# The table of relative biases made in the first stage of a hybrid encoder layer and written to DRAM head by head

## The chip, the cores and the metric

The kernel runs on one core of a Trainium2 chip. The metric is the device time of one execution in microseconds (us). Three runs of the kernel before took 3108.31, 3101.53 and 3108.05 us; the median is 3108.05 us.

## What is computed

One layer with two mixers side by side: a gated delta rule with 16 heads, and a sparse attention with 16 query heads over 2 key and value heads. There are 512 prompt tokens and 64 sample tokens with a past of 1024. Cut to what the change touches:

```python
h = rmsnorm(x, norm_w) * (1.0 + scale[:, None]) + shift[:, None]
proj = h @ w_in                       # 2048 x 16,000 columns, in fp32
(qkv_a, z_a, b_a, a_a, q_b, k_b, v_b, z_b, q_i, k_i, w_i, gl_a, gl_b) = split(proj)

# indexer: scores of all keys, of which the best topk are kept
dots = einsum('bthd,bsd->bths', qi, KI)
score = einsum('bth,bths->bts', wi, relu(dots))
top_val, top_idx = top_k(where(visible, score, -inf), topk)

# attention: the bias depends on the distance of key and query alone
rel = top_idx - q_pos[None, :, None]
bias = rel_bias[rel_bucket(rel)]      # rel_bias is 32 buckets x 16 heads
p = softmax(where(valid, logits + bias, -inf))
o = einsum('btngs,btsnd->btngd', p, Vs)

merged = sigmoid(gl_a) * (o_a @ w_branch_a) + sigmoid(gl_b) * ((o * silu(z_b)) @ w_branch_b)
x = x + gate[:, None] * (merged @ w_out)
```

Keys far enough before the query share the last bucket, so a head's biases are one row of 384 values, shifted by one from query to query, and one constant for keys far away.

## The kernel before

**The tiles.** Every projection is cut into tiles of 128 output columns. A tile loads its weights (`wraw`, 1 MB, line 270, on SP's queue), splits them on ScalarE into a high part (`whi`, line 282) and the negative of it (`wlo`, line 287), and completes the low part by two accumulating transfers of 512 KB each from GpSimd's queue (line 290). `run_tile` (lines 311 to 332) then makes 96 matmuls of 288 columns: 64 of `whi` with the high and the low activations, then 32 of `wlo`. Inside the tile, the weights of the next one are split at the 4th, 14th, 24th and 34th matmul, and those of the third next are loaded at the 84th. The buffers are two deep. In the rows the matmuls are all named `mm`; in the lists of instructions the tile's number stands behind the name (`mm7`, `wraw8`, `whi8`).

**The order.** It is fixed when the program is built. `Plan` keeps a clock of its own for PE (`self.pe`), for each engine and for DMA; each side task is a generator that yields what it waits for, and `tick` runs a task's next step when the plan's clock has come to its due time (lines 129 to 160). `yield 4000` means: 4000 ns later on the plan's clock. These due times only decide in which order instructions are put into the queues. On the chip an instruction starts when its queue has come to it and its semaphores are there.

**SP's queue.** Nearly all transfers are issued by SP, in program order. [...]

**The stages.** The start (adaLN and the normalised activations) is followed by the first stage, `run` from line 1810 on with the pool `p1`: tiles 0 and 1 (keys), 2 (indexer key, `beta` and others), 3 to 10 (indexer queries `qi`), 11 and 12 (values), 13 (a gate). Beside the tiles run `misc` (lines 653 to 743) and the indexer's scores (`score`, lines 817 to 853): nine products `dot` for each of the eight `qi` tiles, through two PSUM buffers that ScalarE empties with a `relu` each. `open_gdn` (line 1730) waits for all of that and opens the delta rule's stage. `open_att` (line 1738) drains the tasks and opens the attention with the pool `p3`.

**The table before.** `bias_setup` (lines 1245 to 1266) is spawned in `open_att`. It loads a one-hot matrix (`oh`) and the 32 by 16 biases (`rb`), makes 16 rows of 512 biases with one product, copies them to SBUF (`f`, named `bf`, 16 partitions), and writes each row's first 384 values 128 times into the DRAM tensor `d_F`, all heads in one transfer (line 1265). Head h's block of keys reads it with a row step of 383 instead of 384, which shifts each row by one (`toeplitz`, line 1268): the tile `BT` in `attend` (line 1311) and `BTs` for the samples (line 1368). `attend` waits for `bias_task` (line 1309). `far` and `fars` hold the constant for far keys. In the attention, `gate_vectors` (line 1477) streams `gada`, 64 pieces of `w_ada`, on the same queue.

Of the kernel before, what the change touches and what calls it, by code (L numbers as in the profile page):

```python
# [7 lines left out]
F32 = mybir.dt.float32  # L8
# [16 lines left out]
H = 16  # L25
# [180 lines left out]
class Kern(Plan):  # L206
# [1037 lines left out]

    def bias_setup(self):

        i, p, V, S = self.i, self.p3, self.V, self.S
        oh = p.tile([32, 512], F32, tag="L3", name="oh", bufs=1)
        S.dma_start(oh, i["k_onehot"])
        rb = p.tile([32, 16], F32, name="rb", bufs=1)  # L1250
        S.dma_start(rb, i["rel_bias"])
        self.far = p.tile([128, 16], F32, name="far", bufs=1)
        S.dma_start(self.far, i["rel_bias"][15:16, :].partition_broadcast(128).rearrange("p a b -> p (a b)"))
        yield [oh, rb, self.far], 9000
        ps = yield from self.tr("biasp")
        self.mm(ps[:16, :], rb, oh)
        f = p.tile([16, 512], F32, tag="PT3", name="bf", bufs=1)
        V.tensor_copy(f, ps[:16, :])
        self.fars = p.tile([128, 8], F32, name="fars", bufs=1)
        v = self.far.rearrange("p (a b) -> p a b", b=2)  # L1260
        for s in range(2):
            V.tensor_copy(self.fars[64 * s:64 * s + 64, :], v[64 * s:64 * s + 64, :, s])
        yield [f]

        S.dma_start(self.d_F, f[:, 0:384].unsqueeze(1).to_broadcast([16, 128, 384]))
        yield [self.d_F]

    def toeplitz(self, h, n, w):

# [36 lines left out]

    def attend(self, a):
        S, p, h = self.S, self.p3, a["h"]
        yield from self.wait(self.kv_task, self.bias_task)
        BT = p.tile([128, 256], F32, tag="BT", name=f"BT{h}")  # L1310
        S.dma_start(BT, self.toeplitz(h, 128, 256))
        yield [BT, a["qT"], a["zt"]]
        yield from self.wait(*[self.spawn(self.attend_block(a, t, BT)) for t in (3, 2, 1, 0)])
        if h % 2:
            a["sample"] = self.spawn(self.attend_sample(h // 2))
# [422 lines left out]
    def open_att(self):  # L1738
        self.drain()
        self.c2.close()  # L1740
        self.c3, self.p3 = self.pool("p3")
        self.slack = 0.0
        self.gpool = lambda: self.p3
        self.bias_task = self.spawn(self.bias_setup())
        self.spawn(self.conv_out())
        self.spawn(self.gate_vectors())
        self.qb_pre(0)()
# [41 lines left out]
    def run(self):  # L1789
        tc = self.tc  # L1790
        with ExitStack() as ctx:
            ctx.enter_context(tc.manual_schedule())
            self.consts(ctx)
            cp = self.cp
            self.wi = cp.tile([128, 4, 16], F32, name="wi")
            self.wis = cp.tile([128, 8], F32, name="wis")
            for n in ("beta", "gc", "egc", "kds"):
                setattr(self, n, cp.tile([128, 5, 16], F32, name=n))
            self.gate = cp.tile([128, KO, 2], F32, name="gate")
            self.diag = cp.tile([128, 64], F32, name="diag")  # L1800
            self.heads, self.att, self.kvT, self.tok = {}, {}, {}, {}
            self.score_tasks, self.topk_task = [], None
            self.topk_gap, self.solve_gap, self.gada_gap = 100, 0, 5000
            self.plan()
            self.hctx = ExitStack()
            pss = self.start(ctx, self.hctx)
            self.catt, self.ap = self.pool("att", bufs=1)
            self.msk = [self.ap.tile([128, 128 * t + 128], F32, name=f"msk{t}") for t in range(4)]
            self.msks = self.ap.tile([128, NS], F32, name="msks")
            self.c1, self.p1 = self.pool("p1")  # L1810
            self.gpool, self.p2 = lambda: self.p1, None
            p = self.p1
            self.kih, self.kil = (p.tile([128, TP + NS], F32R, name=n, bufs=1) for n in ("kih", "kil"))
            self.qss = []
            for b in range(2):
                q = p.tile([128, 2, 128], F32R, name=f"qss{b}", bufs=1)
                self.V.tensor_scalar(q, self.ident.unsqueeze(1).to_broadcast([128, 2, 128]), 0.0, None, op0=ALU.mult)
                self.qss.append(q)
            self.tri = p.tile([128, 2, 128], F32, name="tri", bufs=1)
            self.cache_task = self.spawn(self.cache_idx())  # L1820
            self.load(3)
            for n in range(2):
                for s in range(2):
                    self.stream[n]["epi"](pss[2 * n + s], s)
            self.S.dma_start(self.tri, self.i["k_tri"])
            self.load(4)
            for n in range(2, len(self.stream) - 2):
                self.run_tile(n)
            self.run_last(n + 1)
            self.drain()  # L1830
            for _ in self.finish((2, 3, 4)):
                pass
            for c in (self.c8, self.c6, self.cmg, ):
                c.close()
# [57 lines left out]
```

## Time and profile before

| | |
|---|---|
| median of three runs | 3108.05 us (3101.53 to 3108.31) |
| the profiled execution, whole | 3106.55 us |
| its span, from the first to the last instruction | 3104.8 us |
| PE busy in it | 2972.8 us (96%) |
| VectorE, ScalarE, GpSimd busy | 1389.1, 1542.5, 390.0 us |
| mean granted TensorE clock | 0.977 of full speed |
| first stage, from about | 150 to 357 us |
| attention's opening, about | 1665 to 1750 us |

The profile is of one execution. Its span is 1.75 us shorter than that execution's time. PE is the engine that is nearly always busy, so the time that it stands idle is what other work can cost or give back. In the page's second part the 22nd to 24th of the 40 slices hold the attention's opening.

### The profile page before, as it was taken

The numbers are of one execution on the slowest core, as the hardware profiler recorded it, in microseconds if no ns is written. First come the engines' busy times: TensorE is split into PE (matmuls) and PEld (weight loads), VectorE is DVE, ScalarE is ACT, GpSimd is POOL, SyncE is SP. The second block draws the span as 40 slices with busy tenths as digits, with TensorE's granted clock in tenths as the row PEclk, the third lists the DMA queues.
The fourth block names the chain that finished last, engine by engine and source line by source line (L and its number), as shares of the span: only waits on it lengthen the run. The fifth ranks groups of instructions, "written<-read, shape, count | busy, mean of one in ns | idle before, by whom it ended". The sixth has DMA issues, their size and how long they took to land.

```text
span 3104.8 us, 56419 instructions
## 1 busy us (share of the span) xinstructions
PE 2972.8 (96%) x22363; PEld 2816.3 (91%) x22363; DVE 1389.1 (45%) x4057; ACT 1542.5 (50%) x3332; POOL 390.0 (13%) x727
## 2 busy tenths in 40 slices
PE   6999999999999999999998799999999899999997
PEld 2588999999989989999998699999999899999897
DVE  3334899566667657765651244334422111111112
ACT  3255444555555556665653345444544444444454
POOL 1010111111111111111110000101101111111110
PEclk8999999999999999999999899999999999999999
DMA  9865787766666666676767767776769899888875
GB/s 325 270 147 114 171 185 175 159 162 161 154 144 145 150 145 146 145 167 136 165 153 159 163 160 168 188 177 158 175 148 248 227 234 232 213 209 214 225 159 141
DMA packets 567242, 552.40 MB, mean 178 GB/s; under 512 B 53505, under 2 KB 466066, under 8 KB 565762
## 3 DMA queue, kind: packets, MB, share of 16 engines
q1 hardware_dynamic: 512690, 351.58, 40.1%
q0 software_dynamic: 54144, 197.16, 33.5%
q8 instruction: 176, 2.88, 0.4%
q14 instruction: 88, 0.72, 0.1%
q10 hardware_dynamic: 144, 0.07, 0.0%
HBM read 303.54 MB, written 48.04 MB: 113 GB/s over the span
## 4 chain that ended last, share of the span: by engine, by line
PE 49%; DMA 9%; SPq 3%; ACT 2%; DVE 2%; issue 1%; POOL 0%; ACTq 0%; DVEq 0%; POOLq 0%
PE mm L218 41%; SPq L55 3%; DMA gbl<-d_gb 2%; DMA za<-d_za 2%; DMA wlo<-wraw 2%; PE ob L218 1%; PE lg L218 1%; DMA xf<-in_x_sample 1%; ACT wlo L55 1%; ACT whi L55 1%; PE po L218 1%; PE pT L233 1%; PE obs L218 1%; PE lgs L218 0%; DVE M L55 0%
## 5 line engine op out<-in xcount | busy, mean ns | idle before, releaser
L218 PE MATMUL mm<-hh,whi 128*128 128x288 f32 (+1 forms) x4448 | 1222.3, 301 | 6.1 <-ACT gth L55 5.8
L218 PE MATMUL mm<-hl,whi 128*128 128x288 f32 (+1 forms) x4448 | 1219.8, 300 | 0.0
L218 PEld LDWEIGHTS mm<-hh,whi 128*128 128x128 f32 (+1 forms) x4448 | 839.1, 189 | 22.0 <-issue 9.2
L218 PEld LDWEIGHTS mm<-hl,whi 128*128 128x128 f32 (+1 forms) x4448 | 839.4, 189 | 13.0 <-issue 9.1
L218 PE MATMUL mm<-hh,wlo 128*128 128x288 f32 (+1 forms) x4448 | 685.0, 303 | 4.9 <-DMA wlo<-wraw 4.9
L218 PEld LDWEIGHTS mm<-hh,wlo 128*128 128x128 f32 (+1 forms) x4448 | 619.5, 191 | 13.2 <-DMA wlo<-wraw 5.1
L55 POOL DMA_DIRECT2D wlo<-wraw x376 | 324.3, 863 | 2340.4 <-ACT wlo L55 2062.9
L55 ACT ACTIVATE whi<-wraw 128x512 fp32r<-128x512 f32 x756 | 467.3, 619 | 96.1 <-DMA wraw<-in_w_branch_b 40.2
L55 ACT ACTIVATE wlo<-whi 128x512 fp32r<-128x512 f32 x752 | 475.2, 632 | 70.0 <-PE mm L218 31.6
L55 DVE TENSOR_TENSOR Mt<-M 18x30 f32<-18x30 f32 (+14 forms) x480 | 151.8, 316 | 34.1 <-DMA M<-dN 24.8
L55 DVE TENSOR_TENSOR M<-M,Mt 18x30 f32<-18x30 f32 (+14 forms) x480 | 153.6, 320 | 16.5
L218 PE MATMUL mm<-ga,whi 128*128 128x288 f32 x1024 | 141.1, 297 | 7.1 <-DVE ta L55 6.4
L218 PEld LDWEIGHTS mm<-ga,whi 128*128 128x128 f32 x1024 | 138.3, 190 | 8.2 <-DVE ta L55 7.4
L218 PE MATMUL mm<-mg,whi 128*128 128x288 f32 x1024 | 144.3, 298 | 0.0
L218 PEld LDWEIGHTS mm<-mg,whi 128*128 128x128 f32 x1024 | 139.0, 190 | 0.0
L218 PE MATMUL mm<-gb,whi 128*128 128x288 f32 x1024 | 138.1, 294 | 0.0
L218 PEld LDWEIGHTS mm<-gb,whi 128*128 128x128 f32 x1024 | 136.5, 188 | 0.0
L55 DVE SCALAR_TENSOR_TENSOR cv<-raw,cw,cv 128x579 f32<-128x579 f32 x144 | 117.4, 815 | 4.3 <-ACT cv L55 0.8
L55 DVE SCALAR_TENSOR_TENSOR gacc<-gada,cs,gacc 128x512 f32<-128x512 f32 x120 | 86.6, 744 | 31.1 <-DMA gada<-in_w_ada 31.1
L55 ACT ACTIVATE x<-px 128x128 f32<-128x128 f32 (+1 forms) x80 | 21.9, 274 | 153.4 <-PE px L218 153.4
L55 ACT ACTIVATE raw<-mm 128x288 f32<-128x288 f32 x96 | 36.7, 382 | 99.3 <-PE mm L218 98.4
L55 DVE TENSOR_TENSOR xf<-yp,xf 128x512 f32<-128x512 f32 (+1 forms) x18 | 11.4, 632 | 161.1 <-PE yp L233 134.5
(476 smaller groups left out, 3310.7 us busy)
## 6 DMA issues: line engine op xcount, KB each, us to landing
wlo<-wraw POOLq DMA_DIRECT2D x376, 512.0 KB, 5.4
wraw<-in_w_in SPq DMA_DIRECT2D x140, 1024.0 KB
wa<-in_w_ada SPq DMA_DIRECT2D x64, 512.0 KB
gada<-in_w_ada SPq DMA_DIRECT2D x64, 256.0 KB
wraw<-in_w_branch_a SPq DMA_DIRECT2D x16, 1024.0 KB
wraw<-in_w_branch_b SPq DMA_DIRECT2D x16, 1024.0 KB
wraw<-in_w_out SPq DMA_DIRECT2D x16, 1024.0 KB
d_t<-gth SPq DMA_DIRECT2D x32, 288.0 KB
```

The lines of the kernel that those rows point to most:

```text
L55: r = f(*a, **k)
L218: self.nc.tensor.matmul(out, lhsT, rhs, start=start, stop=stop, **k)
L233: self.nc.tensor.transpose(out, in_, self.ident[:k, :k])
```

## The change

`bias_setup` is spawned in the first stage, before the first tile that `run_tile` handles, and no longer in `open_att`. Its tiles come from the first stage's pool, `far` and `fars` from the constants' pool. The table is written by 16 transfers, one for each head, each from a single partition of `bf`, with a step of 4000 ns on the plan's clock between them. `attend` no longer waits for the task.

```diff
--- before.py
+++ after.py
@@ -1244,26 +1244,26 @@
 
     def bias_setup(self):
 
-        i, p, V, S = self.i, self.p3, self.V, self.S
-        oh = p.tile([32, 512], F32, tag="L3", name="oh", bufs=1)
+        i, p, cp, V, S = self.i, self.p1, self.cp, self.V, self.S
+        oh = p.tile([32, 512], F32, name="oh", bufs=1)
         S.dma_start(oh, i["k_onehot"])
         rb = p.tile([32, 16], F32, name="rb", bufs=1)
         S.dma_start(rb, i["rel_bias"])
-        self.far = p.tile([128, 16], F32, name="far", bufs=1)
-        S.dma_start(self.far, i["rel_bias"][15:16, :].partition_broadcast(128).rearrange("p a b -> p (a b)"))
-        yield [oh, rb, self.far], 9000
+        far = self.far
+        S.dma_start(far, i["rel_bias"][15:16, :].partition_broadcast(128).rearrange("p a b -> p (a b)"))
+        yield [oh, rb, far], 3000
         ps = yield from self.tr("biasp")
         self.mm(ps[:16, :], rb, oh)
-        f = p.tile([16, 512], F32, tag="PT3", name="bf", bufs=1)
+        f = p.tile([16, 512], F32, name="bf", bufs=1)
         V.tensor_copy(f, ps[:16, :])
-        self.fars = p.tile([128, 8], F32, name="fars", bufs=1)
-        v = self.far.rearrange("p (a b) -> p a b", b=2)
+        v = far.rearrange("p (a b) -> p a b", b=2)
         for s in range(2):
             V.tensor_copy(self.fars[64 * s:64 * s + 64, :], v[64 * s:64 * s + 64, :, s])
         yield [f]
 
-        S.dma_start(self.d_F, f[:, 0:384].unsqueeze(1).to_broadcast([16, 128, 384]))
-        yield [self.d_F]
+        for h in range(H):
+            S.dma_start(self.d_F[h], f[h:h + 1, 0:384].unsqueeze(1).to_broadcast([1, 128, 384]))
+            yield 4000
 
     def toeplitz(self, h, n, w):
 
@@ -1306,7 +1306,7 @@
 
     def attend(self, a):
         S, p, h = self.S, self.p3, a["h"]
-        yield from self.wait(self.kv_task, self.bias_task)
+        yield from self.wait(self.kv_task)
         BT = p.tile([128, 256], F32, tag="BT", name=f"BT{h}")
         S.dma_start(BT, self.toeplitz(h, 128, 256))
         yield [BT, a["qT"], a["zt"]]
@@ -1741,7 +1741,6 @@
         self.c3, self.p3 = self.pool("p3")
         self.slack = 0.0
         self.gpool = lambda: self.p3
-        self.bias_task = self.spawn(self.bias_setup())
         self.spawn(self.conv_out())
         self.spawn(self.gate_vectors())
         self.qb_pre(0)()
@@ -1798,6 +1797,8 @@
                 setattr(self, n, cp.tile([128, 5, 16], F32, name=n))
             self.gate = cp.tile([128, KO, 2], F32, name="gate")
             self.diag = cp.tile([128, 64], F32, name="diag")
+            self.far = cp.tile([128, 16], F32, name="far")
+            self.fars = cp.tile([128, 8], F32, name="fars")
             self.heads, self.att, self.kvT, self.tok = {}, {}, {}, {}
             self.score_tasks, self.topk_task = [], None
             self.topk_gap, self.solve_gap, self.gada_gap = 100, 0, 5000
@@ -1817,6 +1818,7 @@
                 self.V.tensor_scalar(q, self.ident.unsqueeze(1).to_broadcast([128, 2, 128]), 0.0, None, op0=ALU.mult)
                 self.qss.append(q)
             self.tri = p.tile([128, 2, 128], F32, name="tri", bufs=1)
+            self.bias_task = self.spawn(self.bias_setup())
             self.cache_task = self.spawn(self.cache_idx())
             self.load(3)
             for n in range(2):
```

In the first stage, SP's queue, which before held between the weights of tiles 5 and 9 (`wraw5` to `wraw9`) only small transfers:

```order
L55 DMA wraw5_1189<-in_w_in 128x16x128
L55 DMA dtb_1237<-in_dt_bias 128x16
L55 DMA dtb_1237<-in_a_log 128x16
L55 DMA out_new_idx_k_prompt<-mt_1226 128x4x64
L55 DMA out_new_idx_k_sample<-mt_1226 64x64
L55 DMA wraw6_1361<-in_w_in 128x16x128
L55 DMA d_g_79<-gr_1429 16x579
L55 DMA wraw7_1566<-in_w_in 128x16x128
L55 DMA wraw8_1755<-in_w_in 128x16x128
```

holds now, in the same place, the sixteen writes of the table:

```order
L55 DMA wraw5_1196<-in_w_in 128x16x128
L55 DMA d_F_87<-bf_1203 128x1x384
L55 DMA dtb_1251<-in_dt_bias 128x16
...
L55 DMA d_F_87<-bf_1203 128x1x384
L55 DMA out_new_idx_k_prompt<-mt_1240 128x4x64
...
L55 DMA d_F_87<-bf_1203 128x1x384
L55 DMA wraw6_1352<-in_w_in 128x16x128
L55 DMA d_F_87<-bf_1203 128x1x384 x4
L55 DMA wraw7_1495<-in_w_in 128x16x128
L55 DMA d_F_87<-bf_1203 128x1x384 x4
...
L55 DMA d_F_87<-bf_1203 128x1x384 x5
L55 DMA wraw8_1733<-in_w_in 128x16x128
```

Three of them stand between `wraw5` and `wraw6`, four between `wraw6` and `wraw7`, and nine (with `d_g` among them) between `wraw7` and `wraw8`. None of the last thirteen has another engine to wait for.

ScalarE's queue within tile 7, where the weights of tile 8 are split, reads in the changed kernel (`relu3_0` and the like empty the products `dot3_0` and the like):

```order
L55 ACTIVATE whi8_1993<-wraw8_1733 128x512
L55 ACTIVATE wlo8_1994<-whi8_1993 128x512
...
L55 ACTIVATE relu3_0_2029<-dot3_0_0_2026 128x512
L55 ACTIVATE relu3_1_2035<-dot3_1_0_2032 128x384
L55 ACTIVATE whi8_1993<-wraw8_1733 128x512
L55 ACTIVATE wlo8_1994<-whi8_1993 128x512
L55 ACTIVATE qi4_2094<-mm7_0_1988 64x288 x2
L55 ACTIVATE relu3_2_2104<-dot3_2_0_2101 128x256
```

Three pairs of the split stand ahead of `relu3_0` (one is shown), one behind `relu3_1`; in the kernel before these rows stood in the same order.

At the attention's opening, SP's queue held before

```order
L55 DMA gada2_19620<-in_w_ada 128x512
L55 DMA d_F_87<-bf_19643 2048x1x384
L55 DMA gada3_19706<-in_w_ada 128x512
L55 DMA wraw99_19757<-in_w_in 128x16x128
L55 DMA gada4_19777<-in_w_ada 128x512
L55 DMA BT0_19790<-d_F_87 128x256
```

and holds now

```order
L55 DMA gada2_19639<-in_w_ada 128x512
L55 DMA wraw98_19644<-in_w_in 128x16x128
L55 DMA gada3_19722<-in_w_ada 128x512
L55 DMA wraw99_19772<-in_w_in 128x16x128
L55 DMA BT0_19791<-d_F_87 128x256
L55 DMA gada4_19795<-in_w_ada 128x512
```

The write of the table is gone from it, and the first head's read, `BT0`, stands right behind the weights of tile 99.

## Rows read from the trace of the kernel before

**Rows 1.** the page: the span, and part 1, busy us (share of the span)

```profile
span 3104.8 us, 56419 instructions
...
PE 2972.8 (96%) x22363; PEld 2816.3 (91%) x22363; DVE 1389.1 (45%) x4057; ACT 1542.5 (50%) x3332; POOL 390.0 (13%) x727
```

**Rows 2.** waits of PE over the whole span: us in total, times, longest us

```profile
PE lg L218 <- DVE L L55: 18.0, 4, 17.5
...
PE mm L218 <- DMA wlo<-wraw: 4.9, 1, 4.9
```

**Rows 3.** timeline of SP as the attention opens: start us, us, issue

```profile
1691.20 0.62 SPq L55 DMA_DIRECT2D d_F<-bf  x1
1691.88 7.94 SPq L55 DMA_DIRECT2D gada<-in_w_ada  x1
...
1734.59 0.38 SPq L55 DMA_DIRECT2D BT<-d_F  x1
```

**Rows 4.** DMA issues, 1685 to 1740 us: count, KB each

```profile
d_F<-bf SPq DMA_DIRECT2D x1, 3072.0 KB
```

**Rows 5.** timeline of DVE, the two rows behind the transfer

```profile
1734.73 1.41 DVE L55 SCALAR_TENSOR_TENSOR gacc<-gada,cs,gacc 128x512 f32<-128x512 f32 x2 [30.29 <-DMA gada<-in_w_ada]
1739.15 0.76 DVE L55 SCALAR_TENSOR_TENSOR L<-lg,BT 128x256 f32<-128x256 f32 x2 [3.00 <-issue]
```

**Rows 6.** timeline of PE, 1711 to 1746 us

```profile
1711.69 0.29 PE L218 MATMUL mm<-hl,whi 128*128 128x288 f32 x1
1716.86 2.05 PE L218 MATMUL mm<-hh,wlo 128*128 128x288 f32 x7 [4.88 <-DMA wlo<-wraw]
...
1739.63 1.22 PE L218 MATMUL lg<-KT,qT 128*128 128x256 f32 x2 [17.51 <-DVE L L55]
...
1745.90 0.29 PE L218 MATMUL mm<-hh,whi 128*128 128x288 f32 x1
```

**Rows 7.** busy time of tile lg alone, the next head

```profile
1767.00:1773.00 6.00, 2.75 (x8) 1.32 (x8) 1.44 (x4) 0.84 (x2) 1.00 0.87 163
```

**Rows 8.** stretches: us, PE, PEld, DVE, ACT, POOL busy (x), PEclk, DMA share, GB/s

```profile
167.00:215.00 48.00, 48.00 (x321) 42.78 (x320) 20.20 (x55) 29.34 (x62) 5.34 (x8) 1.00 0.61 128
1693.00:1707.00 14.00, 14.00 (x108) 14.00 (x107) 1.51 (x3) 5.10 (x11) 1.39 (x3) 1.00 0.89 102
1710.00:1726.00 16.00, 7.24 (x30) 5.27 (x28) 0.00 (x0) 0.84 (x2) 0.00 (x0) 0.75 1.03 174
1736.00:1740.00 4.00, 0.37 (x1) 0.37 (x2) 0.90 (x3) 0.00 (x0) 0.00 (x0) 0.50 1.04 310
1740.00:1750.00 10.00, 10.00 (x59) 9.82 (x59) 6.34 (x25) 5.55 (x15) 0.00 (x0) 0.73 0.32 85
3096.50:3099.50 3.00, 0.00 (x0) 0.00 (x0) 0.00 (x0) 0.00 (x0) 0.00 (x0) 0.50 1.03 407
3101.00:3102.30 1.30, 0.00 (x0) 0.00 (x0) 0.00 (x0) 0.00 (x0) 0.00 (x0) 0.50 0.98 205
```

**Rows 9.** DMA queues, 1710 to 1726 us: packets, MB, share

```profile
q0 software_dynamic: 525, 1.92, 69.1%
q1 hardware_dynamic: 549, 0.84, 33.7%
```

**Rows 10.** timeline of SP in the first stage, one load of a tile's weights

```profile
163.69 0.39 SPq L55 DMA_DIRECT2D wraw<-in_w_in  x1
```

**Rows 11.** timeline of SP at the end of the program

```profile
3081.24 16.07 SPq L55 DMA_DIRECT2D out_y_prompt<-xf  x8
3097.40 2.52 SPq L55 DMA_DIRECT2D out_y_sample<-xf  x2
```

**Rows 12.** timeline of PE, first matmul of the eighth tile

```profile
237.77 0.29 PE L218 MATMUL mm<-hh,whi 128*128 128x288 f32 x1
```

**Rows 13.** groups of ACT, 200 to 240 us: busy us, mean ns

```profile
L55 ACT ACTIVATE wlo<-whi 128x512 fp32r<-128x512 f32 x8 | 5.1, 632 | 0.3
L55 ACT ACTIVATE whi<-wraw 128x512 fp32r<-128x512 f32 x8 | 5.0, 624 | 0.0
```


## The prediction

> **What bounds the kernel now.** First the page: PE is busy for 96% of a span of 3104.8 us [rows 1], so a change is worth what it takes from or adds to the time in which PE stands still. Next the waits of PE over the whole span: the longest single one is 17.5 us, of the product `lg` on VectorE's `L`, and 4.9 us stand beside it for `wlo`, a tile's low weights [rows 2]. Both lie in one place, so the timelines of that place come third. SP issues the table's write, 3072 KB, at 1691.20 us and the first head's read `BT` only at 1734.59 [rows 3, 4]. VectorE adds the bias to `L` at 1739.15 [rows 5], and PE, which had run its last `whi` matmul of that tile at 1711.69, goes on at 1739.63 and begins the next tile at 1745.90 [rows 6]. Last come the stretches, for what the transfer does meanwhile: from 1693 to 1707 the DMA engines are 0.89 busy and move only 102 GB/s [rows 8].
>
> **What the change takes away.** From 1711.8 to 1745.9 PE needs 34.1 us. In that time it does 32 matmuls of `wlo` and the head's `lg`. A matmul takes 0.13 us (108 of them in the 14 us from 1693 [rows 8]), and `lg` 2.75 us in the next head, where nothing holds it up [rows 7]. That is 7.0 us of work and 27.1 us of loss, the slow clock behind the stall (0.73 from 1740 to 1750 [rows 8]) included. Without the write this goes: the accumulating transfers of the tile and `gada` no longer stand behind it. What is late next is `BT0`, issued behind 1 MB of weights (3.4 us at the 310 GB/s of 1736 to 1740 [rows 8]). The plan now puts 39 matmuls, 5 us, between it and the first use of its head, so I count nothing for it; at most 3 us stay. Gain: 27.1 us, bounded by 24 and 27.1. The product for the table, its copy and the three small loads move from one stage to the other and cancel. The two tiles in the constants' pool cost 96 bytes a partition and no instruction.
>
> **What it adds.** The same 3072 KB go out in the first stage, 192 KB (196.6 thousand bytes) for each head, and each transfer reads a single partition. The 4000 ns between them exist on the plan's clock alone. In SP's queue they come in groups: three between `wraw5` and `wraw6`, four up to `wraw7`, nine, around `d_g`, up to `wraw8`. SP's transfers are served in order: `gada`, issued at 1691.88 right behind the table, reached VectorE at 1734.73 [rows 3, 5]. So whatever time the 16 transfers take, the weights of tile 8 come behind all of it.
>
> How long does one take? No row shows a transfer from one partition. The nearest rows are those of stores with all DMA engines busy (0.89 to 1.03): from 128 partitions, the prompt's output, 407 GB/s; from 64, the sample's output, 205; from 16, the table, 102 [rows 8, 11]. The rate falls with the number of partitions but not in proportion: a quarter of the partitions, from 64 to 16, halves it. Bounds: if 102 GB/s belongs to the form of the transfer and not to its partitions, a head takes 1.93 us; if a partition gives no more alone than as one of 16 (6.4 GB/s), it takes 30.7 us. I carry the last step on, two more quarters and two more halves: 25.5 GB/s, 7.7 us. This is near the geometric middle of the two ends and the only one of the three values that follows the trend of the rows.
>
> The Trainium skill has a price for this place. Its page "SBUF — State Buffer", section "Door 1: The DMA port swizzle", says that a transfer's rate goes with how many of 16 ports its partitions reach, that four neighbouring partitions share one port, and that 0..3 gave 27.6 GB/s, 0..15 104 and 0..63 196. The trace agrees where it can (102 and 205 GB/s); that one partition reaches what its port gives no run here shows. By it a head would take 7.1 us and the sum below would end at 3135 us.
>
> The sum. `wraw5` is issued at 163.69 us [rows 10]; 1 MB behind that, at 167.3, the table's transfers begin. Until the weights of tile 8 have landed, the queue needs 16 x 7.7 = 123.4 us for the table and 3 x 3.4 = 10.2 us for three loads. The accumulating transfers of tiles 5 to 7, six of 512 KB, run on the same DMA engines from the other queue. From 1710 to 1726 they moved 1.92 MB, and the table 0.84 instead of the 1.63 MB that 102 GB/s would have made in 16 us [rows 9]: 0.79 MB or 7.7 us lost, so 4.0 us for each MB and 12.6 us for six. Here the DMA engines mostly wait for one partition and can do that work in between, so it costs 0 to 12.6; I take half, 6.3. `wraw8` lands at 167.3 + 123.4 + 10.2 + 6.3 = 307.2 us.
>
> Who waits: ScalarE's queue is in order. In tile 7 three pairs of the split of `wraw8` stand ahead of the first `relu` of that tile, 1.25 us a pair [rows 13]. PE can issue two products `dot3` into the two buffers and 82 matmuls, and then stands before `dot3_2`. Up to tile 7 PE has the same work in both kernels, and the tile begins at 237.77 [rows 12]; 82 matmuls (0.13 us each, 10.7) and two products (four matmuls, half of the 2.75 us of `lg`'s eight [rows 7], 1.4) later it is 249.9 us. It goes on at 307.2 + 3 x 1.25 = 311.0. Loss: 61.1 us. `wraw7`, behind seven of the transfers, holds PE in the same way in tile 6, but that is time it would wait later anyway. Behind such a stall the granted clock stays at the lower of its two levels (1.2 and 2.4 GHz) for a while: 0.50 in the idle stretch up to 1740, and 0.73 on the mean over the next 10 us, so (1 - 0.73) x 10 = 2.7 us [rows 8]. Nothing behind gives this back, for PE is the bound of the following stages; the end of the first stage comes later by as much.
>
> Together: - 27.1 + 61.1 + 2.7 = + 36.7 us. The profiled execution took 3106.55 us (1.75 us around its span), so 3143.2; the median of the runs is 1.5 us above that execution: 3145 us.
>
> **Rivals.**
> 1. *Hidden altogether.* 102 GB/s is what such a store reaches, from 16 partitions or one. Then 16 x 1.93 = 31 us lie beside a first stage whose DMA share is 0.61 at 128 GB/s [rows 8]; in the 70 us until tile 8's weights are wanted at 238 the engines have 0.39 x 70 = 27 us free, about the 0.89 x 31 = 28 us of the table, and only the gain is left: 3106.55 - 27.1 + 1.5 = 3081 us, faster. For it speak the room, and that the trace has the 102 GB/s for rows of the same 1536 bytes; against it that stores of other rows go at 205 and 407 with the engines no busier, so it is not the store that is slow.
> 2. *One partition gives no more than its share of 16*, 6.4 GB/s. 16 x 30.7 = 491 us; PE stands until 167.3 + 491 + 10.2 + 6.3 + 3.8 = 678.6 instead of 249.9, and the time is about 3512 us. For it: 64 and 128 partitions give the same 3.2 GB/s each, so rates in proportion do occur; against it: 16 give 6.4 each, so a partition can give more when fewer are read.
> 3. *The two sides cancel.* The loss equals the gain where 16 t = 27.1 - 2.7 + 249.9 - 3.8 - 6.3 - 10.2 - 167.3 = 86.7, at t = 5.4 us a head or 36 GB/s. That is the point from which the forecast's sign turns. A rate there would need half as much again as the trend gives; 3108 us.
>
> **Chances.** The forecast 0.67, rival 1 0.20, rival 2 0.08, rival 3 0.05. The forecast's own range takes 23 to 28 GB/s (8.5 and 7.0 us a head) and 0 to 12.6 us for the accumulating transfers: a loss of 43 to 83 us less the 27.1, so 3124 to 3164 us. The range that is to hold 8 in 10 reaches down over rivals 3 and 1 with 3 to 5 us below the latter, and up a little over the forecast's end: 3076 to 3172. A run of this kernel tells 0.3% (9 us) from no change. Faster: rival 1 and a little, 0.21. Within 0.3%: 0.05. Slower: 0.74.
>
> **What would show it.** In the profile after: (1) the wait of `lg` on `L` near 1700 us and the long `gada` issues are gone, and `BT0` lands in a few us; (2) in the stretch from 167 to about 310 us, the DMA engines are busy at some 25 to 60 GB/s, and `wraw8` lands near 307; (3) PE has one or two waits in the first stage, behind ScalarE's split or `relu` and so behind `wraw7` and `wraw8`, of about 60 us together, with a low granted clock behind them; (4) the first stage ends by that much later and everything between it and the attention lies as before. It is wrong if the table's transfers land in 2 us each and PE is never idle in the first stage after 167 us, or if each takes 15 us and more.

## The result: 3149.7 us, 1.4% slower, and the profile after

| | before | after |
|---|---|---|
| median, us (runs) | 3108.2 (3101.5 to 3109.9) | 3149.7 (3143.7 to 3152.9) |
| ratio, 95% interval | | 1.0139 [1.0120, 1.0159] |
| profiled execution, us | 3106.55 | 3143.67 |
| its span, us | 3104.8 | 3141.9 |
| TensorE idle, 160 to 440 us (280 less its busy time) | 0.4 | 49.3 |

Of all profiles below, that of `e4_four_spread` alone was taken in an execution with a mean granted clock of 0.79 (3381.7 us); only the rate of a transfer is read from it.

The waits of PE over the whole span come first (us in total, times, longest us), against [rows 2]:

```profile
PE dot L218 <- ACT relu L55: 38.6, 2, 31.2
...
PE mm L218 <- DMA wlo<-wraw: 9.4, 3, 4.9
PE z L218 <- DMA TT<-dX: 8.8, 11, 3.9
```

The 17.5 us of `lg` on `L` have gone, and 31.2 us stand elsewhere: a product `dot` waits for ScalarE's `relu`. SP's timeline of the first stage shows what is ahead of it (start us, us, issue); of before, [rows 10] has one such load:

```profile
213.79 7.48 SPq L55 DMA_DIRECT2D wraw<-in_w_in  x1
221.32 25.98 SPq L55 DMA_DIRECT2D d_F<-bf  x4
247.41 11.67 SPq L55 DMA_DIRECT2D d_g<-gr  x1
259.13 27.55 SPq L55 DMA_DIRECT2D d_F<-bf  x5
286.88 15.25 SPq L55 DMA_DIRECT2D wraw<-in_w_in  x2
```

SP stands at its issues for about as long as the transfers ahead take, and the weights of tile 8 are issued at 286.88. The chain of waits follows them to PE (start us, us, what):

```profile
286.88 18.76 DMA wraw<-in_w_in
...
309.34 0.61 ACT relu L55
...
309.99 1.09 PE dot L218 x2
```

They land at 305.64, three pairs of the split and one `relu` follow, and the product starts at 309.99. In the kernel before, the same product was at 250.08:

```profile
250.08 0.28 PE L218 MATMUL dot<-kih,qi 128*128 128x256 f32 x1
```

The stretches, beside those of [rows 8] (us, PE, PEld, DVE, ACT, POOL busy (x), PEclk, DMA share, GB/s), one of the kernel before first, then those after:

```profile
160.00:440.00 280.00, 279.58 (x1926) 260.22 (x1925) 171.43 (x356) 149.55 (x299) 30.73 (x39) 1.00 0.67 152
```
```profile
160.00:440.00 280.00, 230.67 (x1454) 207.81 (x1455) 113.68 (x276) 121.01 (x249) 22.59 (x28) 0.89 0.76 118
283.00:297.00 14.00, 0.00 (x0) 0.00 (x0) 0.00 (x0) 0.00 (x0) 0.00 (x0) 0.50 0.85 27
310.00:320.00 10.00, 10.00 (x45) 7.99 (x46) 4.56 (x10) 5.99 (x15) 0.86 (x1) 0.74 0.78 158
310.00:440.00 130.00, 130.00 (x852) 118.72 (x853) 79.65 (x192) 70.53 (x143) 14.65 (x17) 0.98 0.65 146
```

From 283 to 297 only transfers of the table run: the DMA engines are 0.85 busy and move 27 GB/s. PE stands still meanwhile, and the granted clock is at the lower of its two levels (0.50, 1.2 GHz).

Where the 37.1 us of the span lie is read from one row of each kernel, ScalarE's copy `oT`, which runs from the first head of the GDN part to its last (op, count: ns min/median/max, first and last start us); first before, then after:

```profile
L55 ACT ACTIVATE oT<-ot x80: 292/310/328, 591.9 to 1661.1; 128x128 f32<-128x128 f32 x64, 64x128 f32<-64x128 f32 x16
```
```profile
L55 ACT ACTIVATE oT<-ot x80: 292/312/326, 655.0 to 1730.4; 128x128 f32<-128x128 f32 x64, 64x128 f32<-64x128 f32 x16
```

Up to the first of them the change loses 63.1 us; between first and last another 6.2 (1075.4 for 1069.2); from the last to the end it gains 32.2 (1411.5 for 1443.7).

### The profile page after: what moved, and what is told of

It reads as the page before. It is cut to its first block, busy times and chain, and to the rows that moved or that the text cites. A ratio compares the mean times of both kernels' runs of the same rounds, so it can differ in the third digit from the quotient of the medians.

```text
span 3141.9 us, 56451 instructions
## 1 busy us (share of the span) xinstructions
PE 2985.9 (95%) x22363; PEld 2828.8 (90%) x22363; DVE 1389.3 (44%) x4057; ACT 1542.5 (49%) x3332; POOL 390.6 (12%) x727
## 4 chain that ended last, share of the span: by engine, by line
PE 75%; DMA 11%; SPq 4%; DVE 4%; ACT 3%; issue 2%; POOL 0%; ACTq 0%; DVEq 0%; POOLq 0%
PE mm L218 61%; SPq L55 4%; DMA za<-d_za 2%; DMA wa<-in_w_ada 2%; DMA gbl<-d_gb 2%; PE ob L218 1%; PE lg L218 1%; ACT wlo L55 1%; PE ada L218 1%; PE po L218 1%; ACT whi L55 1%; DVE M L55 1%; PE dot L218 1%; DMA xf<-in_x_sample 1%; DMA TT<-dX 1%
## 5 line engine op out<-in xcount | busy, mean ns | idle before, releaser
L218 PEld LDWEIGHTS mm<-hh,wlo 128*128 128x128 f32 (+1 forms) x4448 | 621.8, 191 | 20.4 <-DMA wlo<-wraw 10.2
```

Source lines behind the costliest of these rows:

```text
L218: self.nc.tensor.matmul(out, lhsT, rhs, start=start, stop=stop, **k)
```

## The experiments

The theory: a transfer from one partition moves some 27 GB/s, 7.1 us a head; what stands in one row ahead of a tile's weights makes them late by as much, and nothing else of the change costs anything. Its rivals: the count doesn't matter, or the rate is one of the form of the transfer, or one-partition transfers take time from the weights wherever they stand. "Idle" is TensorE's idle time from 160 to 440 us, as in the table above, and `e1` to `e11` stand for the labels that begin so. Ratios are to the kernel before.

**The two halves of the change apart.** The table in the first stage, but in one transfer from 16 partitions:

```
-        for h in range(H):
-            S.dma_start(self.d_F[h], f[h:h + 1, 0:384]...to_broadcast([1, 128, 384]))
-            yield 4000
+        S.dma_start(self.d_F, f[:, 0:384].unsqueeze(1).to_broadcast([16, 128, 384]))
+        yield 4000
```

> Place alone: the table is made in the first stage but written in one transfer from 16 partitions. Theory 'rate' (a store from one partition runs at some 27 GB/s, one from 16 at 102, and what stands behind it in SP's queue waits): 31 us of transfer between wraw5 and wraw6; wraw6 and the accumulating transfers of tile 5 come 10 to 15 us late, the attention's 27 us are gone: 3085 to 3100 us, faster than before. Theory 'place' (any table in the first stage holds its weights up): as slow as the change, 3150. Theory 'order' (the moved PE and ScalarE rows of the first stage cost the time): also near 3150.

Measured: 3113.6 us, 1.0027 [1.0012, 1.0043], idle 18.6; a miss, 14 us over the range. The attention's gain is there (26 us from the last `oT` to the end), the first stage was not free. The chain of waits and the stretch:

```profile
175.75 28.13 DMA dtb<-in_a_log
```
```profile
170.00:190.00 20.00, 17.93 (x135) 17.70 (x133) 3.64 (x13) 6.43 (x15) 1.71 (x2) 1.00 0.91 112
```

The table goes out at some 102 to 112 GB/s, as in [rows 8], but the two small loads of the decay (`dtb`) stand behind it. They land at 203.9, and ScalarE's first work on them, `ea`, starts there instead of at 172.2; VectorE's `g` waits for them, ScalarE waits behind the first of that chain with the next tile's split, and PE for both (`gcp` on `g` 10.1 us, `mm` on `wlo` 8.0). I had counted the weights alone as what is queued behind.

Head by head, but at the old place, in the kernel before:

```
-        S.dma_start(self.d_F, f[:, 0:384].unsqueeze(1).to_broadcast([16, 128, 384]))
-        yield [self.d_F]
+        for h in range(H):
+            S.dma_start(self.d_F[h], f[h:h + 1, 0:384]...to_broadcast([1, 128, 384]))
+            yield 4000
```

> Form alone: the table is made where it was before, as the attention opens, but written head by head. Theory 'rate': 16 x 7.1 us = 114 us in SP's queue in place of 38, with wraw99 to wraw101 and BT0 behind it; PE stands some 85 us there in place of 27: 3150 to 3185 us. Theory 'place': the 16 small transfers let the others pass, so no slower than before, 3085 to 3108.

Measured: 3187.5 us (two runs), 1.0257 [1.0223, 1.0291], a little over the range. The wait of PE, and one of the stretches in it:

```profile
PE lg L218 <- DVE L L55: 82.2, 3, 81.8
```
```profile
1780.00:1790.00 10.00, 0.00 (x0) 0.00 (x0) 1.37 (x2) 0.00 (x0) 0.00 (x0) 0.50 0.85 27
```

27 GB/s again, in another stage. The change's form costs more than its place gives.

**The count.** 24 transfers instead of 16, the further ones into a table that nothing reads:

```
...
+            if h < 8:
+                S.dma_start(self.d_F2[h], f[h:h + 1, 0:384]...to_broadcast([1, 128, 384]))
```

> The changed kernel with 8 more one-partition transfers (24 in place of 16; the 8 go to a scratch table that nothing reads, one behind each of the first 8 heads). If the loss is the queue's length in front of the next weight tiles, each transfer adds its 7.1 us: 8 x 7.1 = 57 us over the changed kernel, 3207 us (3195 to 3215). If the loss is a fixed stop (one late load, one clock fall) that the count doesn't set: within 15 us of the changed kernel's 3150 us.

Measured: 3203.9 us, 1.0317 [1.0288, 1.0345], idle 101.8. Eight transfers more cost 54.2 us over the change, 6.8 us each (by the two ratios and their intervals 5.6 to 8.3). A stop of a fixed length is excluded.

**Which partitions.** Four transfers of four heads each, at the same places in SP's queue; once of four neighbours, once of four that are 4 apart:

```
...
+        for g in range(4):
+            S.dma_start(self.d_F[4 * g:4 * g + 4], f[4 * g:4 * g + 4, 0:384]...)    # neighbours
+            S.dma_start(self.d_F[g:16:4], f[g:16:4, 0:384]...)                      # 4 apart
+            yield 16000
```

> The changed kernel, but the table leaves in 4 transfers of 4 neighbouring partitions each (heads 0..3, 4..7, 8..11, 12..15), one ahead of each of four successive weight tiles. Two readings of the 7.1 us per head: (a) the neighbours share one way out of SBUF: each transfer then takes 4 x 7.1 = 28 us, some 114 us in all stand ahead of the weight tiles, and about 40 us of them show: 3124 us (3115 to 3140), DMA rate in 170-290 us near 27 GB/s; (b) each partition alone has 27 GB/s: four in parallel give some 105 GB/s, a transfer takes 7.5 us and is hidden: 3081 to 3092 us.

> The same 4 transfers at the same places, each of 4 partitions that are 4 apart (heads g, g+4, g+8, g+12). Both readings of the 7.1 us per head (neighbours share a way out; each partition has its own rate) give four ways at once, some 100 GB/s and 7 to 8 us a transfer, hidden behind the matmuls: 3076 to 3092 us. A third reading, that a transfer spread over few partitions is slow whichever they are, gives the time of the neighbours, some 3124 us.

Measured: neighbours 3154.2 us, 1.0156 [1.0137, 1.0174], idle 62.2; 4 apart 3097.0 us, 0.9964 [0.9944, 0.9983], 5 us above its range but on its side. A stretch with the table's transfer nearly alone, first of the neighbours, then of those 4 apart:

```profile
188.00:192.00 4.00, 0.00 (x0) 0.00 (x0) 0.00 (x0) 0.00 (x0) 0.00 (x0) 0.50 0.23 26
```
```profile
222.00:225.00 3.00, 3.00 (x19) 2.93 (x18) 1.30 (x4) 1.21 (x4) 0.00 (x0) 0.75 0.29 106
```

The same bytes in the same number of transfers at 26 and 106 GB/s. Four neighbours together give what one of them gives alone (27): they share what limits them, four that are 4 apart do not. The busy share of the DMA engines isn't it: at 0.85 they moved 27 GB/s for one partition, at 0.23 they moved 26 for four neighbours, at 0.29 they moved 106. The two kernels also differ in which rows of the table are written together; that the rows written are not what is slow is seen in `e7` below, which writes the same table from another source. The time of the neighbours lies 14 us above my range. A transfer of 28 us stands ahead of `dtb`, as in the first experiment: VectorE's first work on `dtb` starts at 207.47 us, after 29.9 us without work, and PE loses 29.1 us there before the decay's `gcp`, beside 31.3 us at `dot`:

```profile
PE dot L218 <- ACT relu L55: 31.3, 2, 17.3
PE gcp L218 <- issue: 29.1, 1, 29.1
```

**In order, or overlapping.** The change's 16 transfers with the heads in the order 0, 4, 8, 12, 1, 5, ...:

```
-        for h in range(H):
+        for n in range(H):
+            h = 4 * (n % 4) + n // 4
```

> The changed kernel with the heads in the order 0, 4, 8, 12, 1, 5, ..: neighbouring transfers leave from partitions 4 apart; order, count and places of the transfers are those of the change but for one. If a queue takes its transfers strictly one after the other, nothing changes: 3140 to 3155 us, plateau 27 GB/s. If neighbouring transfers overlap as far as their ways out of SBUF differ, the plateau rises to 50 to 100 GB/s, and the time falls to 3085 to 3115 us.

Measured: 3107.8 us, 1.0007 [0.9992, 1.0022], idle 20.6: the overlapping it is. SP issues the weights of tile 8 at 256.41 instead of 286.88, and a stretch with table transfers alone shows more than twice the rate:

```profile
256.41 77.46 SPq L55 DMA_DIRECT2D wraw<-in_w_in  x6
```
```profile
250.00:258.00 8.00, 6.94 (x53) 6.71 (x51) 0.00 (x0) 0.00 (x0) 0.00 (x0) 1.00 0.76 61
```

The order of the heads alone is worth 41.9 us of the change's time (3149.7 to 3107.8).

**Where they stand.** The plan books each transfer on a DMA clock, by `4 * n * out.shape[0]` bytes (line 98), `n` being the largest product of an operand's sizes without the first. A head's broadcast row of [1, 128, 384] into a table of 128 rows counts there as 4 x 49152 x 128 = 25 MB, 128 times its bytes. Three kernels with the transfers issued past that booking, two of them with the pace changed too (what the expectations call a column is a nanosecond of the plan's clock):

```
-            S.dma_start(self.d_F[h], ...)
-            yield 4000
+            self.nc.sync.dma_start(self.d_F[h], ...)    # not booked
+            yield 12000                                 # 4000 in e8, 9000 in e10
```

> The change with its 16 transfers really spread: the transfer is left out of the plan's account (which books 128 times its bytes) and the step is 12000 ns, so one or two stand between the weights of each tile from 5 to 16. Theory 'rate': each still takes 7.1 us at 27 to 29 GB/s, but a tile of 17 us has room for one; nothing is late in the first stage and the attention's 27 us are gone: 3076 to 3090 us. Theory 'number' (16 transfers cost time whatever stands behind them): near 3150.

Measured: 3131.4 us, 1.0078 [1.0057, 1.0099], idle 10.0; a miss. The first stage is nearly free, but the task is not finished where the GDN part opens, and `open_gdn` joins all tasks but the top-k search before it emits more. Meanwhile the search alone is put into VectorE's order. The search's rows, here and in `e7` below, which has no such delay:

```profile
L55 DVE MAX8 max8s<-msks x32: 1277/1286/1287, 401.3 to 489.4; 64x8 f32<-64x1088 f32 x32
```
```profile
L55 DVE MAX8 max8s<-msks x32: 1271/1284/1289, 395.6 to 520.1; 64x8 f32<-64x1088 f32 x32
```

The 32 steps take 88 us in one piece instead of 125 with the GDN part's work between them, and that work starts later: ScalarE's first write of `raw` is at 480.3 us against 445.9. PE waits for it:

```profile
PE mm L218 <- ACT raw L55: 13.8, 1, 13.8
```

PE's idle time is 10.0 us up to 440 us and another 16.2 from 440 to 500, where `e7` has none in either. What makes up the rest of the 44.6 us between the two kernels was not settled. That the open task is the cause fits the next kernel, which differs in the pace alone: its task ends earlier, and the loss is gone.

> The changed kernel, heads one by one, with the transfers left out of the plan's DMA clock and 9000 columns between them, so that one or two stand ahead of each weight tile and the last is issued before the attention keys' rows are stored, ahead of the point where the GDN part opens and joins all tasks. If the loss was only where the transfers stand (thirteen ahead of one weight tile) and the spaced run's 3131 us came from the join, the whole loss goes and the attention's gain shows: 3076 to 3092 us. If one-partition transfers cost the weights time wherever they stand: 3120 to 3135 us as spaced over 12000.

Measured: 3085.2 us (ten runs, 3077.3 to 3106.5), 0.9939 [0.9918, 0.9961], idle 2.4: faster than both kernels. One or two transfers ahead of each tile's weights are hidden altogether; the stretch, and two loads of SP with the heads between them:

```profile
200.00:350.00 150.00, 150.00 (x955) 133.03 (x955) 67.73 (x150) 86.27 (x179) 13.79 (x16) 1.00 0.85 124
```
```profile
282.60 0.37 SPq L55 DMA_DIRECT2D wraw<-in_w_in  x1
283.02 2.24 SPq L1265 DMA_DIRECT2D d_F<-bf  x2
306.58 0.38 SPq L55 DMA_DIRECT2D wraw<-in_w_in  x1
```

The same pace with the booking left in:

```
-            yield 4000
+            yield 9000
```

> The changed kernel with 9000 columns in place of 4000 between the heads, the transfers booked on the plan's DMA clock as in the change (the spaced run that ended by 345 us differs from this one by the booking alone). If the booking (each head at 128 times its bytes) sets where they stand, ten still stand in one row ahead of one weight tile: 3140 to 3155 us, as the change. If the pace sets it: 3080 to 3095 us.

Measured: 3148.8 us, 1.0144 [1.0119, 1.0169], idle 48.7, as the change. With the booking, ten heads stand in one row at this pace too:

```profile
211.00 71.96 SPq L55 DMA_DIRECT2D d_F<-bf  x10
283.14 42.69 SPq L55 DMA_DIRECT2D wraw<-in_w_in  x4
```

And the change's 4000 without the booking:

> The changed kernel with its 4000 columns, the transfers left out of the plan's DMA clock: three or four stand ahead of each of five weight tiles. By lengths of the queue: 16 x 7.1 + 5 loads x 3.4 = 131 us over some 5 tiles x 18 us = 90 us, less the buffers' lead of 18 us: 23 us of TensorE lost, 3081 + 23 = 3104 us (3095 to 3115). If only a long row of transfers hurts: 3080 to 3090. If the pace of the plan alone sets the loss: 3140 to 3155.

Measured: 3125.0 us, 1.0072 [1.0053, 1.0090], idle 27.7; a miss, 10 us over the range. The idle time came near the 23 us of the estimate, the time did not: the median is 39.8 us over that of the kernel with 9000. The execution of `e10` that was profiled is 8 us above its median, so the two profiles are only 31.2 us apart. In them the first head's `oT` comes 36.0 us later here than in `e10` (635.4 and 599.4). Idle time is 25.3 of these, and the low granted clock around the stops, (1 - PEclk) x busy time over stretches of 10 us from 160 to 440, some 8 (10.8 less 3.0); I had priced the stops alone. Three loads land 24 to 25 us after their issue (in the chain of waits), and each stops PE. First that chain, then a stretch behind the first of them, then `oT` here and in `e10`:

```profile
217.25 24.24 DMA wraw<-in_w_in
...
248.09 25.20 DMA wraw<-in_w_in
...
274.88 24.76 DMA wraw<-in_w_in
```
```profile
240.00:250.00 10.00, 4.17 (x11) 2.82 (x12) 2.01 (x4) 6.55 (x12) 1.72 (x2) 0.50 0.85 42
```
```profile
L55 ACT ACTIVATE oT<-ot x80: 292/311/327, 635.4 to 1708.0; 128x128 f32<-128x128 f32 x64, 64x128 f32<-64x128 f32 x16
```
```profile
L55 ACT ACTIVATE oT<-ot x80: 292/311/323, 599.4 to 1675.6; 128x128 f32<-128x128 f32 x64, 64x128 f32<-64x128 f32 x16
```

**Without the one partition.** The 16 rows are first written to a small table in DRAM, and the large one is filled from that, DRAM to DRAM:

```
...
+        S.dma_start(self.d_f, f[:, 0:384])
+        yield [self.d_f]
+        S.dma_start(self.d_F, self.d_f.unsqueeze(1).to_broadcast([16, 128, 384]))
```

> Source alone: in the first stage the 16 rows go to DRAM once (24 KB) and the table is then written from there in one transfer, DRAM to DRAM, with no SBUF partition read. Theory 'rate': if it is the partitions read that limit the rate, this runs at 200 GB/s or more, 16 us or less, is hidden, and the time is 3076 to 3090 us, the best of all. If stores of 1536-byte rows of this table are slow in themselves, it takes 31 us again and ends with e1, 3085 to 3100.

Measured: 3086.9 us, 0.9933 [0.9915, 0.9952], idle 0.0: as fast as the well-spaced heads, with two transfers and no pace to choose. From 170.5 us, where the copy is issued, to 186 SP's queue alone moved 3.00 MB, nearly the table's bytes; so writing the table's rows is not what limits the rate. A stretch that holds part of the copy and a tile's weights:

```profile
180.00:190.00 10.00, 10.00 (x78) 9.45 (x78) 2.28 (x8) 7.04 (x14) 1.80 (x3) 1.00 1.08 318
```

## Why the prediction was right, and where its steps were off

**In sum.** Forecast: -27.1 for the attention and +63.8 for the first stage with the clock behind it. Measured: -32.2, +63.1, and +6.2 in the GDN part, which the sum had at nothing. So the large term was right, and that the total came within 5 us owes something to luck, as the paragraphs below show.

**The gain of the attention: right in its cause, too small.** 27.1 us were forecast, with 24 and 27.1 as bounds; from the last `oT` to the end it is 32.2 us in the change, above them, and 24 to 32 in nine further kernels with an early table (all but `e4`; 27.7 in `e7`). The wait of `lg` for `L` went from 18.0 us to 0.5. Where the further 5 us come from was not tried.

**The rate of one partition: a little low, and near by luck.** Forecast 7.7 us a head (25.5 GB/s); the plateau of 27 GB/s gives 7.3, the count of 24 gives 6.8. The ends, 1.93 and 30.7 us, are excluded, and rivals 1 and 2 with them. The trend of the rows from 128, 64 and 16 partitions led to a number that is nearly right, but the reason was wrong: the rate does not go by the count of partitions. Halved with each quarter, four partitions would give 51 GB/s and one 25.5; measured, four neighbours give 26, no more than one, and four others 106, as many as sixteen (102). The Trainium skill's page "SBUF — State Buffer", section "Door 1: The DMA port swizzle", has four neighbours on one port and 27.6 GB/s for it; the runs agree, with 26 to 27 for one partition and for four neighbours and 106 for four ports.

**The queue up to `wraw8`: right in sum, two terms off.** Forecast 307.2 us, measured 305.64. The 16 transfers took 6 to 14 us less than the 123.4 (16 x 7.3 or 16 x 6.8), and what is left for the accumulating transfers and the rest (305.6 - 167.3 - 10.2 less 117 or 109) is 11 to 19 us instead of 6.3, where 0 to 12.6 were allowed for. What that remainder consists of was not taken apart.

**The stop of PE: right in its end, not in its shape.** Forecast: one loss of 61.1 us, from 249.9 to 311.0. Measured: the product that was at 250.08 before is at 309.99, 59.9 us later. But PE had stood still several times on the way (5 us at 190 to 200, some 7 at 230 to 250, 35.6 from 270 to 310), 49.3 us in all; of the other 11 us some 7 lie around the stops, where the granted clock was 0.66 to 0.83 in stretches of 10 us ((1 - PEclk) x busy time); the last 4 are not accounted for. Since the queue sets the end, it makes no difference how PE spends the time until then, as the prediction said of `wraw7`.

**The clock behind it: right.** 2.7 us were forecast, and (1 - 0.74) x 10 = 2.6 us stand in the stretch from 310 to 320; in the kernel before, the clock there is 1.00.

**"Everything in between as before": not quite.** The GDN part took 6.2 us more, and the attention's gain was 5.1 us larger than forecast; that the two cancel is luck. In eight further kernels with an early table (all but `e4` and `e9`) the GDN part took 1069 to 1077 us, and 1069 to 1070 in the two with a late one. PE's waits for `TT` grew from 3.0 to 8.8 us; what makes them was not tried, and stays open.

**The signs and the range.** Sign (2) asked for 25 to 60 GB/s in the whole stretch from 167 to about 310 us. It was 84: beside the table the stretch holds three loads and six accumulating transfers, which by the sum's own terms make 67 on the mean. Only where the table went out alone was it 27. Of the forecast's own range the upper end, 83 us of loss, contains the 2.7 us of the clock and the lower, 43, does not; with it the range begins at 3127 us instead of 3124, and the measured time lies inside either way.

**What the prediction didn't see.** It took the row of nine heads ahead of `wraw8` as it found it in the order (the thirteen of one expectation above are these and the four ahead of `wraw7`). That the row is an effect of the booking, and that the heads' order is worth 42 us, was left to the runs. "Served in order" holds nearly for the change, where most consecutive heads lie in neighbouring partitions, which share what limits them; in `e5`, where they do not, consecutive transfers overlap.

## What to carry to other kernels

Price a transfer by the partitions that it reads: split by neighbouring partitions, a store that took some 31 us takes some 115, and behind it in the queue stands every load that an engine is about to need, the smallest too. Before splitting, ask for a source that has no such limit (here DRAM itself). Where a plan spaces transfers by a clock of its own, look at what it books for each: here the same transfers lost 1.4% where thirteen stood ahead of two loads, and won 0.6% spread out.

## What the runs showed of the hardware

- A broadcast store of 1536-byte rows from one SBUF partition moved 27 GB/s at a DMA share of 0.85 (the change, `e2`); four neighbours in one transfer moved 26 at 0.23 (`e3`), four that are 4 apart 106 at 0.29 (`e4`).
- Consecutive transfers of one queue overlapped: with sources 4 partitions apart the queue moved 61 GB/s (`e5`) where the same transfers in the order of the partitions moved 27 (the change).
- The same table from DRAM to DRAM was hidden behind PE's work (`e7`, no idle time), with 318 GB/s in a stretch of 10 us together with a tile's weights.
